# Gate tiles with the expert of a group innermost in place of the token

## The chip, the core and the metric

The kernel runs on one core of one Trainium2 chip. The metric is the device time of one execution, in microseconds (us). Three runs of the kernel before took 4170.88 us at the median, 4170.69 at the least and 4181.73 at the most.

## The reference

Two layers of a hybrid network run over 640 tokens of 1024 numbers (128 context tokens, 512 latent ones). Each layer has a mixer and then PEER, an expert layer with 16384 experts of one neuron each. For each token and each of 8 heads it takes the 16 best of all pairs of two keys (128 x 128 pairs are the 16384 experts), a softmax over these 16 gives the gates, and the output is a sum over the 128 chosen experts:

```
sv, si = lax.top_k(s, PEER_TOPK)                 # 16 best of 128 keys, for both halves
cand = sv[:, :, 0, :, None] + sv[:, :, 1, None, :]
fv, fpos = lax.top_k(cand, PEER_TOPK)            # 16 best of the 256 pairs
eidx = take_along_axis(cidx, fpos)               # number of the expert, i * 128 + j
g = softmax(fv)
act = gelu(einsum('td,ted->te', xb, u_tab[idx]))
out = einsum('te,ted->td', g * act, v_tab[idx])
```

## The kernel before, in words

PEER is done in two ways at once. For two tiles of 128 tokens the rows of `u` and `v` that the tokens chose are gathered from DRAM (`gather`, lines 1043 to 1065): an indirect DMA that GpSimd issues fetches 128 rows of 4 KB into one of four buffers `gb`, and VectorE takes a product with it or adds it to `acc`. For the other three tiles, 384 tokens, all 16384 experts are computed (`dense`, from line 1251): 128 blocks i of 128 experts j, each a product with `u` (tile `A`), a multiplication by the gates, and a product with `v`. Most gates are zero. The gathered rows are spread over the other stages in small portions, in the order in which the code is written, so that GpSimd, VectorE and the DMA queues work on them beside the matmuls.

The change is in the dense gates. The matrix of gates is 128 (j, on partitions) by 128 (i) by 384 tokens, in 16 groups of 8 blocks i. The first 4 groups (`NRES`) are kept in SBUF in the tile `Gt` (named `GT` in the code), the other 12 are spilled to the DRAM tensor `g_d` by way of the tile `Gs`, which has three buffers. Both have been laid out so far as group, block of 16 tokens, i in the group, token, the token innermost.

The gate stage (`gate`, lines 1210 to 1249) takes 16 tokens a step, in two halves of 8. For each half, TensorE makes `pj` and `pi` (lines 1222 and 1226), ScalarE and VectorE turn them into one-hot rows `OJ` and `OI` (lines 1223 and 1237; each fourth `OI` goes over ScalarE at line 1234 and GpSimd), and two groups of four products `pg` (line 1242) give the gates of four tokens each, a row of 128 numbers (over i) per token in PSUM. ScalarE evicts each group of four with two copies: 128 numbers into `Gt` (line 1244) and 384 into `Gs` (line 1246). It reads them in the order token, i. After 16 tokens SyncE issues the store of `Gs` to `g_d` (line 1248), 12 runs of 128 numbers on each partition. Beside it the last parts of the selection of other tiles run on VectorE and GpSimd (`late`, in the first 8 steps of the gate stage for one tile and in the first 9 steps of the dense stage for another), and one portion of gathered rows per half.

In the dense stage step i loads the weights, forms `A` for block i (`upd`), and for block i - 1 multiplies `A` by the gates (`mid`, lines 1277 to 1284), splits the product into a high part (ScalarE) and a low part (VectorE) in `wp`, and runs 18 matmuls with `v` (`down`, line 1293); `up` (line 1144) has 24. The product with the gates is line 1281, and a helper at line 77 records it:

```
av = A.rearrange("p (b t) -> p b t", t=16)
mul(av, av, GT[:, i // 8 % NRES, :, i % 8])
```

From the 32nd block on, a group of `Gt` that has been used is filled again from `g_d` (line 1259). In the last layer a used part of `Gt` holds rows of the output's gate (`final_rows`).

Each engine works through its instructions in the order in which the program lists them; the order is fixed when the program is built, and semaphores make an engine wait for another.

Of the kernel before, what the change touches and what calls it, by code (L numbers as in the profile page):

```python
# [20 lines left out]
D = 1024  # L21
# [22 lines left out]
def tile_kernel(ctx: ExitStack, tc: tile.TileContext, I, O, dbg=None, upto=99):  # L44
# [65 lines left out]
    # some columns of a modulation at a time: the weights stream past the two conditioning columns  # L110
# [50 lines left out]
    # pre: the first weights, split before  # L161
# [24 lines left out]
    # sums of the squares of the rows of xT, in two parts  # L186
# [12 lines left out]
    # 1 / rms of the tokens, on all partitions, in PSUM  # L199
# [78 lines left out]
    # an angle of any size modulo 2 pi, into [-pi, pi]  # L278
# [15 lines left out]
    # =========================== Hyena filters ===========================  # L294
    # Transforms at the odd frequencies 2 pi (f + 1/2) / 2L. For the latent tokens the even and the odd samples are
    # transformed apart, into E and O: what belongs to f is E + O, and the conjugate of what belongs to L - 1 - f
    # is E - O.
# [4 lines left out]
    # the discrete Fourier matrices come in two parts that float32r holds exactly  # L302
# [106 lines left out]
    # =========================== layer 0 mixer ===========================  # L409
# [19 lines left out]
    with ExitStack() as eq:  # L429
# [47 lines left out]
        # the input is read again after this: its place holds the convolved rows and the sum of the states  # L477
# [138 lines left out]
    # activations of one table follow each other  # L616
# [6 lines left out]
    def rglru(cp):  # L623
        # 4 softplus(-lambda), log1p by its atanh series
# [46 lines left out]
        def scans(d):  # L671
            for j in range(4):
# [3 lines left out]
                # q = (1 + a) / 2 = 1 / (1 + p), refined by one Newton step; its negative is kept  # L676
# [29 lines left out]
    # what the first direction of the S5 layer needs early  # L706
# [33 lines left out]
    with es, ExitStack() as eb:  # L740
# [6 lines left out]
        # the places of the convolved rows and of the states' sum are free again  # L747
# [76 lines left out]
        # what the chunks put out for four pairs of groups: from the chunk itself and from the state before it  # L824
# [88 lines left out]
    # =========================== PEER ===========================  # L913
# [7 lines left out]
    g_d = [dram.tile([16, 128, TD // 16, 8, 16], F32, name=f"g_d{l}") for l in range(2)]  # L921
# [34 lines left out]
    def peer(l):  # L956
# [5 lines left out]
        # the scores of two token tiles wait for their turn  # L962
# [22 lines left out]
        # one head of the n token tiles at slot s0: its 16 of the 54 pairs that can be among the largest  # L985
# [161 lines left out]
        # the first blocks of experts need no gates yet  # L1147
# [6 lines left out]
        GT = rp.tile([128, NRES, TD // 16, 8, 16], F32, name="Gt")  # L1154
# [19 lines left out]
        # dense gate matrix of a token tile: G[i][j, t], by one-hot products per token  # L1174
        # The numbers of a slot's two keys, each as digits a and b of 4 bits, make the row of a product whose
        # column c is 1 - (a - a_c)^2 - (b - b_c)^2: what is left above 0 is the one-hot row of the key.
# [33 lines left out]
        def gate(n, cr, gT, it, lt):  # L1210
            for tb in range(8):
                next(lt, None)
                Gs = kp.tile([128, 128 - 8 * NRES, 16], F32, name="Gs", tag="Gs", bufs=NGS)
                for t8 in range(2):
# [24 lines left out]
                    for t4 in range(2):  # L1239
# [4 lines left out]
                        S.copy(GT[:, :, tr, :, c0:c0 + 4].rearrange("p r i t -> p t r i"),  # L1244
# [6 lines left out]
        def dense(lp):  # L1251
# [25 lines left out]
            def mid(i):  # L1277
                A = st["A", i]
                WH, WL = wp[:, i % 2, 0], wp[:, i % 2, 1]
                av = A.rearrange("p (b t) -> p b t", t=16)  # L1280
                mul(av, av, GT[:, i // 8 % NRES, :, i % 8])
                S.copy(WH, A)  # L1282
                sub(WL, A, WH.bitcast(F32))
                st["W", i] = WH, WL
# [459 lines left out]
```

## Time and profile before

The profiled execution has a span of 4170.6 us, which is all that the profile gives as its own time; the three timed runs stand beside it.

| what | value |
|---|---|
| median of the runs | 4170.88 us |
| span of the profiled execution | 4170.6 us |
| TensorE matmul busy | 3630.2 us (87%) |
| VectorE busy | 3420.7 us (82%) |
| GpSimd busy | 2632.5 us (63%) |
| ScalarE busy | 1690.0 us (41%) |
| mean granted TensorE clock | 0.935 |
| DMA, mean over the span | 254 GB/s |

The shares are means over stages with different limits: the mixers, the selection, the gate stage and the dense stage. Engines are PE (TensorE matmul), PEld (its weight loads, which overlap the matmuls), DVE (VectorE), ACT (ScalarE), POOL (GpSimd) and SP (SyncE). What a number in the table is worth for the change is read from the stage in which the changed instructions run. The times of matmuls overlap, since one starts before the last has ended; so do those of ScalarE's and VectorE's instructions in part, and an instruction's duration is longer than the time for which it holds up the next.

### The profile page before, as it was taken

What the parts mean: (1) busy time and instruction counts of PE and PEld (TensorE: products, weight loads), DVE (VectorE), ACT (ScalarE), POOL (GpSimd) and SP (SyncE); (2) the same over time, 40 slices, a digit from 0 to 9 for tenths busy, and PEclk for the clock granted to TensorE, in tenths of its full rate; (3) what the DMA queues carried; (4) which work ended last, traced back from release to release, by engine and by line L of the source; (5) the groups of instructions that cost most, each with busy time, mean ns of one, the idle gap of its engine ahead of it and who ended that gap; (6) DMA issues with size and microseconds to landing.
All of it is one profiled execution on the core that took longest, in us unless ns stands there. A gap on an engine that the chain in (4) does not pass through costs nothing.

```text
span 4170.6 us, 57304 instructions
## 1 busy us (share of the span) xinstructions
PE 3630.2 (87%) x20066; PEld 3161.8 (76%) x20098; DVE 3420.7 (82%) x5990; ACT 1690.0 (41%) x3488; POOL 2632.5 (63%) x2178
## 2 busy tenths in 40 slices
PE   7868887488999999999789988843889999999997
PEld 4656873367898898998678778732678999999986
DVE  8872599989888888889865666999888888888888
ACT  3523435494333333333344333444843333333333
POOL 5631588757666666666655435887576666666675
PEclk9978998799999999999889999977999999999998
DMA  5564267698898999999724642656878999899997
GB/s 207 140 134 145 92 207 223 203 293 272 308 344 323 339 328 338 340 327 329 250 81 127 218 132 87 208 163 187 283 267 315 340 339 348 324 341 338 330 323 246
DMA packets 438105, 1057.42 MB, mean 254 GB/s; under 512 B 49175, under 2 KB 210967, under 8 KB 432696
## 3 DMA queue, kind: packets, MB, share of 16 engines
q0 software_dynamic: 152784, 555.55, 38.4%
q1 hardware_dynamic: 285032, 498.21, 35.5%
q8 instruction: 158, 2.59, 0.2%
q14 instruction: 131, 1.07, 0.1%
HBM read 993.86 MB, written 61.87 MB: 253 GB/s over the span
## 4 chain that ended last, share of the span: by engine, by line
PE 38%; DVE 26%; DMA 13%; issue 10%; POOL 7%; ACT 6%; SPq 1%; POOLq 0%; DVEq 0%; ACTq 0%
PE pso L1293 13%; PE pA L1144 12%; DMA gb<-in_peer_v,ei 8%; PE pproj L169 8%; DVE gb L1052 6%; POOL gb L1040 4%; DVE acc L95 3%; ACT Gs L1246 2%; DMA gb<-in_peer_u,ei 2%; PE pmod L129 2%; POOL jk L77 1%; DVE oh L77 1%; DVE ul L77 1%; ACT OJ L1223 1%; DVE tiu L976 1%
## 5 line engine op out<-in xcount | busy, mean ns | idle before, releaser
L1040 POOL DMA_INDIRECT gb<-in_peer_v,ei x512 | 687.9, 1343 | 435.0 <-DVE acc L95 335.6
L1293 PE MATMUL pso<-vh,wp 128*128 128x512 f32 x3072 | 883.3, 395 | 32.5 <-ACT wp L1282 23.9
L95 DVE SCALAR_TENSOR_TENSOR acc<-gb,pw,acc 128x1024 f32<-128x1024 f32 x508 | 774.4, 1524 | 137.0 <-DMA gb<-in_peer_v,ei 132.9
L1040 POOL DMA_INDIRECT gb<-in_peer_u,ei x512 | 636.0, 1242 | 391.3 <-DVE gb L1052 257.8
L1052 DVE SCALAR_TENSOR_TENSOR gb<-gb,hrow 128x1024 f32<-128x1024 f32 x512 | 756.1, 1481 | 100.8 <-DMA gb<-in_peer_u,ei 100.3
L1144 PE MATMUL pA<-hHd,uh 128*128 128x384 f32 x2048 | 691.6, 338 | 12.9 <-DVE modT L77 6.2
L1144 PE MATMUL pA<-hHd,ul 128*128 128x384 f32 x2048 | 691.6, 338 | 4.4 <-DVE ul L77 4.4
L1144 PE MATMUL pA<-hLd,uh 128*128 128x384 f32 x2048 | 690.0, 337 | 0.0
L1293 PEld LDWEIGHTS pso<-vh,wp 128*128 128x128 f32 x3072 | 575.1, 189 | 151.1 <-ACT wp L1282 29.5
L1293 PE MATMUL pso<-vl,wp 128*128 128x512 f32 x1536 | 486.8, 396 | 15.5 <-POOL vl L77 13.9
L1136 ACT CAST uh<-wraw 128x1024 fp32r<-128x1024 f32 x256 | 269.4, 1052 | 457.9 <-PE pA L1144 444.8
L1282 ACT CAST wp<-A 128x384 fp32r<-128x384 f32 x252 | 129.5, 514 | 781.1 <-DVE A L77 767.6
L1144 PEld LDWEIGHTS pA<-hHd,uh 128*128 128x128 f32 x2048 | 387.6, 189 | 24.3 <-DVE modT L77 6.2
L1144 PEld LDWEIGHTS pA<-hHd,ul 128*128 128x128 f32 x2048 | 387.3, 189 | 8.4 <-DVE ul L77 6.6
L1144 PEld LDWEIGHTS pA<-hLd,uh 128*128 128x128 f32 x2048 | 387.3, 189 | 8.2
L1293 PEld LDWEIGHTS pso<-vl,wp 128*128 128x128 f32 x1536 | 291.8, 190 | 83.2 <-POOL vl L77 15.2
L77 POOL TENSOR_TENSOR wl<-wraw,wh 128x1024 fp32r<-128x1024 f32 (+1 forms) x88 | 215.8, 2455 | 205.4 <-ACT wh L157 194.4
L77 DVE TENSOR_TENSOR ul<-wraw,uh 128x1024 fp32r<-128x1024 f32 x252 | 314.2, 1247 | 36.8 <-ACT uh L1136 33.5
L77 POOL TENSOR_TENSOR vl<-vraw,vh 128x1024 fp32r<-128x1024 f32 x128 | 332.3, 2596 | 15.8 <-ACT vh L1266 12.3
L1266 ACT CAST vh<-vraw 128x1024 fp32r<-128x1024 f32 x256 | 268.9, 1050 | 160.1 <-PE pso L1293 74.7
L1242 PEld LDWEIGHTS pg<-OI,OJ 128*128 128x128 f32 x1536 | 202.5, 202 | 112.4 <-POOL OI L77 42.8
L1242 PE MATMUL pg<-OI,OJ 128*128 128x128 f32 x1536 | 222.1, 292 | 43.9 <-DVE OI L1237 18.9
(537 smaller groups left out, 7020.1 us busy)
## 6 DMA issues: line engine op xcount, KB each, us to landing
wraw<-in_uT SPq DMA_DIRECT2D x256, 512.0 KB
vraw<-in_peer_v SPq DMA_DIRECT2D x256, 512.0 KB
g_d<-Gs SPq DMA_DIRECT2D x48, 768.0 KB
Gt<-g_d SPq DMA_DIRECT2D x24, 1536.0 KB
wmod<-in_w_mod SPq DMA_DIRECT2D x48, 512.0 KB
wraw<-in_wq SPq DMA_DIRECT2D x32, 512.0 KB
mw<-in_w_mod SPq DMA_DIRECT2D x16, 1024.0 KB
wraw<-in_w_in_c SPq DMA_DIRECT2D x24, 512.0 KB
```

The source lines that it names most:

```text
L77: (eng or V).tensor_tensor(o, a, b, op=op)
L95: V.scalar_tensor_tensor(o, a, s, b, op0=op0, op1=op1)
L129: PE.matmul(pm[:2, :cw], cond[:, k], w[k], start=k == 0, stop=k == 7)
L169: PE.matmul(p[:, i, :sg[2]], a[:, k, :], sg[hl](k), start=k == 0 and a is wh and hl == 0, stop=k == kk - 1 and a is wl)
L1040: G.indirect_dma_start(out=b, out_offset=None, in_=I[tab], in_offset=bass.IndirectOffsetOnAxis(ap=ei[:, s:s + 1], axis=0))
L1052: V.scalar_tensor_tensor(b, b, 1.0, hrow[:, i], op0=ALU.mult, op1=ALU.mult, accum_out=act[:, s:s + 1])
L1136: S.copy(uh, u)
L1144: PE.matmul(pA, a[:, k], b[:, k], start=k == 0 and b is hHd and a is uh, stop=k == 7 and a is ul)
L1242: PE.matmul(pg[:, t], OJ[:, t4 * 4 + t], OI[:, t4 * 4 + t], start=True, stop=True)
L1266: S.copy(vh, v)
L1282: S.copy(WH, A)
L1293: PE.matmul(pso[n][h], a[:, c], b[:, h * 512:(h + 1) * 512], start=i == 0 and a is WH and b is vh, stop=i == 127 and a is WL)
```

## The change

In `Gt`, `Gs` and `g_d` the last two dimensions change places: group, block of 16 tokens, token, i in the group. So the 8 numbers i of a group stand side by side for one token, where before 16 tokens stood side by side for one i. The two evictions read the same numbers in the same order and write them to the new places; they stand in a loop on one line now. The product with the gates reads its 384 numbers 8 places apart.

```diff
-    g_d = [dram.tile([16, 128, TD // 16, 8, 16], F32, name=f"g_d{l}") for l in range(2)]
+    g_d = [dram.tile([16, 128, TD // 16, 16, 8], F32, name=f"g_d{l}") for l in range(2)]
...
-        GT = rp.tile([128, NRES, TD // 16, 8, 16], F32, name="Gt")
+        GT = rp.tile([128, NRES, TD // 16, 16, 8], F32, name="Gt")
...
-                Gs = kp.tile([128, 128 - 8 * NRES, 16], F32, name="Gs", tag="Gs", bufs=NGS)
+                Gs = kp.tile([128, 16 - NRES, 16, 8], F32, name="Gs", tag="Gs", bufs=NGS)
...
-                        S.copy(GT[:, :, tr, :, c0:c0 + 4].rearrange("p r i t -> p t r i"),
-                               pg[:, :, :NRES * 8].rearrange("p t (r i) -> p t r i", i=8))
-                        S.copy(Gs[:, :, c0:c0 + 4].rearrange("p i t -> p t i"), pg[:, :, NRES * 8:])
+                        for o, a in ((GT[:, :, tr], pg[:, :, :NRES * 8]), (Gs, pg[:, :, NRES * 8:])):
+                            S.copy(o[:, :, c0:c0 + 4].rearrange("p r t i -> p t r i"),
+                                   a.rearrange("p t (r i) -> p t r i", i=8))
                     take(it, WSLOT[gi % len(WSLOT)])
-                nc.sync.dma_start(g_d[l][NRES:, :, n * 8 + tb].rearrange("g p i t -> p g (i t)"),
-                                  Gs.rearrange("p (g i) t -> p g (i t)", i=8))
+                nc.sync.dma_start(g_d[l][NRES:, :, n * 8 + tb].rearrange("g p t i -> p g (t i)"),
+                                  Gs.rearrange("p g t i -> p g (t i)"))
...
-                mul(av, av, GT[:, i // 8 % NRES, :, i % 8])
+                mul(av, av, GT[:, i // 8 % NRES, :, :, i % 8])
...
-            grow = GT[:, 0].rearrange("p b i t -> p (b i t)")[:, :2 * D].rearrange("p (s d) -> p s d", s=2)
+            grow = GT[:, 0].rearrange("p b t i -> p (b t i)")[:, :2 * D].rearrange("p (s d) -> p s d", s=2)
```

On TensorE, VectorE, GpSimd and SyncE the instructions stand in the same order before and after. On ScalarE they do too, with the evictions in another form. Before, a piece of ScalarE's order in the gate stage of layer 0 reads (`Gt` and `Gs` are the evictions, `OJ` and `OI` the one-hot rows):

```order
L1244 COPY Gt<-pg 128x4x4x8
L1246 COPY Gs<-pg 128x4x96
L1223 ACTIVATE OJ<-pj 128x1024
L1244 COPY Gt<-pg 128x4x4x8
L1246 COPY Gs<-pg 128x4x96
L1234 ACTIVATE OI<-pi 128x512
```

The same place after the change:

```order
L1245 COPY Gt<-pg 128x4x4x8
L1245 COPY Gs<-pg 128x4x12x8
L1223 ACTIVATE OJ<-pj 128x1024
L1245 COPY Gt<-pg 128x4x4x8
L1245 COPY Gs<-pg 128x4x12x8
L1234 ACTIVATE OI<-pi 128x512
```

Nothing has moved; `Gs` is written as 4 tokens by 12 groups by 8, and both evictions have one line.

## Rows read from the trace of the kernel before

**Rows 1.** Windows, gate stage: stretch, length, PE, PEld, DVE, ACT, POOL busy (count), clock, DMA share, GB/s.
```profile
763.00:863.00 100.00, 68.91 (x382) 51.73 (x389) 100.00 (x322) 60.78 (x109) 77.29 (x128) 0.86 0.63 191
880.00:938.00 58.00, 55.91 (x396) 44.16 (x401) 42.85 (x71) 58.00 (x111) 29.06 (x30) 1.00 1.02 328
...
2978.00:3030.00 52.00, 50.13 (x354) 39.55 (x359) 38.16 (x64) 52.00 (x100) 25.84 (x27) 1.00 1.03 321
```

**Rows 2.** Chain of waits, gate stage's second halves: start, duration, what.
```profile
865.02 0.65 ACT Gs L1246
...
938.65 1.07 ACT Gs L1246
...
2959.69 0.65 ACT Gs L1246
...
3030.71 1.05 ACT Gs L1246
```

**Rows 3.** Timeline of SyncE's queue, 880 to 940 us: first start, stretch, what, count.
```profile
879.92 58.40 SPq L1248 DMA_DIRECT2D g_d<-Gs  x11
```

**Rows 4.** Timeline of ScalarE, gate stage: start, duration, what.
```profile
897.92 0.51 ACT L1244 COPY Gt<-pg 128x128 f32<-128x128 f32 x1
...
898.75 0.76 ACT L1234 ACTIVATE OI<-pi 128x512 f32<-128x512 f32 x1
899.26 0.51 ACT L1244 COPY Gt<-pg 128x128 f32<-128x128 f32 x1
```

**Rows 5.** Timeline of TensorE, the same place.
```profile
897.69 1.05 PE L1242 MATMUL pg<-OI,OJ 128*128 128x128 f32 x8
898.58 0.59 PE L1222 MATMUL pj<-blk,cr 128*128 128x512 bf16 x2
```

**Rows 6.** Single lines, ScalarE's copies out of PSUM: duration in ns, min/median/max.
```profile
L1246 ACT COPY Gs<-pg x192: 801/902/1122, 770.7 to 3044.3; 128x384 f32<-128x384 f32 x192
...
L1103 ACT COPY sc<-psc x32: 451/479/509, 490.2 to 2753.5; 128x384 f32<-128x384 f32 x32
...
L1207 ACT COPY gT<-pgT x6: 246/258/273, 737.5 to 2943.3; 128x128 f32<-128x128 f32 x6
...
L466 ACT COPY uT<-pproj x8: 689/734/807, 127.1 to 175.7; 128x320 f32<-128x320 f32 x8
```

**Rows 7.** Single lines, TensorE's matmuls of the gate stage.
```profile
L1242 PE MATMUL pg<-OI,OJ x1536: 270/275/579, 769.3 to 3043.7; 128*128 128x128 f32 x192
...
L1222 PE MATMUL pj<-blk,cr x166: 376/379/634, 764.9 to 3031.5; 128*128 128x512 bf16 x166
```

**Rows 8.** Windows, dense stage, as rows 1.
```profile
950.00:1100.00 150.00, 134.51 (x629) 119.10 (x630) 139.18 (x195) 51.60 (x69) 116.28 (x99) 0.93 0.81 277
1100.00:1900.00 800.00, 793.30 (x3992) 719.36 (x3992) 680.09 (x746) 277.75 (x379) 508.66 (x335) 1.00 0.92 334
...
3730.00:3780.00 50.00, 50.00 (x254) 45.44 (x253) 44.88 (x60) 17.51 (x24) 31.17 (x22) 1.00 0.95 358
```

**Rows 9.** Groups by form, VectorE: total us, mean ns, idle before.
```profile
L77 DVE TENSOR_TENSOR A<-A,Gt 128x384 f32<-128x384 f32 x252 | 149.0, 591 | 0.1
...
L1017 DVE TENSOR_REDUCE ef<-jk 128x16 f32<-128x432 f32 x48 | 42.1, 877 | 2.0 <-POOL jk L77 2.0
...
L1026 DVE TENSOR_REDUCE gs<-gt 128x8 f32<-128x128 f32 x4 | 1.1, 278 | 0.3 <-ACT gt L1025 0.3
...
L1026 DVE TENSOR_REDUCE gs<-gt 128x24 f32<-128x384 f32 x2 | 1.1, 542 | 0.0
```

**Rows 10.** Waits, 950 to 2090 us: who for whom, us in total, times, longest.
```profile
DVE acc L95 <- DMA gb<-in_peer_v,ei: 63.1, 54, 4.5
...
PE pso L1293 <- ACT wp L1282: 13.4, 9, 4.6
```

**Rows 11.** Chain of waits through the run: products with the gates on it.
```profile
953.10 0.93 DVE Apre L77 x2
...
4129.60 0.56 DVE A L77
```

## The prediction

> **What bounds the kernel now.** I read the windows of busy time first, to find the stages in which the changed instructions run, then the chain of waits inside them, then the times of single instructions. The changed instructions run in two places of each PEER layer.
>
> The first is the gate stage (763 to 945 us in layer 0, 2862 to 3045 us in layer 1). It has two halves with different limits. In the first half VectorE is busy for the whole of its 100 us and ScalarE for 61 of them; in the second ScalarE is busy for 58.00 of 58 and 52.00 of 52 us, VectorE for under three quarters [rows 1]. The chain agrees: in the second half it runs through the evictions `Gs` on ScalarE, from 865.0 to 939.7 us and from 2959.7 to 3031.8 us [rows 2], 147 us in all. SyncE's stores give the pace there: 11 in a row, ten steps between 879.92 and 937.96 us, 5.80 us a step of 16 tokens [rows 3]. So 147 us are 25 steps whose pace ScalarE sets.
>
> The second place is the dense stage (950 to 2050 and 3036 to 4130 us). Its middle is TensorE's: 793 of 800 us busy, VectorE 680 [rows 8]. A step of one expert block has 42 matmuls, so the 3992 of that row are 95 steps of 8.4 us, in each of which VectorE is idle for 120 / 95 = 1.26 us. At the stage's beginning and end VectorE is tighter (139 of 150 us) [rows 8].
>
> **The change part by part.** No instruction, wait or transfer is added, removed or moved; each store still moves 12 runs of 128 numbers a partition. Two kinds of instruction get other strides.
>
> *The evictions.* For every 4 tokens ScalarE copies 512 numbers out of PSUM, 128 into `Gt`, 384 into `Gs`. Before, two numbers read one after another are written 64 bytes apart; now eight in a row are written together. Copies that write in a row take 258 ns for 128 numbers and 479 for 384: 0.86 ns a number over a base of 148. `Gs` takes 902 for the same 384, (902 - 148) / 384 = 1.96 a number, and `uT`, the other copy that scatters its writes, takes 734 for 320, 1.83 [rows 6]. What an instruction holds the engine for is read from its successor's start: `Gt` and `Gs` together 898.75 - 897.92 = 0.83 us, the 512-wide `OI` behind them, written in a row, 0.51 [rows 4]. If eight in a row are as good as a full row, ScalarE saves 4 x (0.83 - 0.51) = 1.28 us of the 5.80, and needs 4.5.
>
> What is late next? TensorE: eight product matmuls stand in 1.05 us with the last of 0.275 [rows 5, 7], so one starts every (1.05 - 0.275) / 7 = 0.111 us; two wide ones stand in 0.59 us, the last of 0.379, 0.211 apart [rows 5, 7]. [...] The DMA queues come close behind: the stretch moves 328 GB/s [rows 1], 1.90 MB a step. At the most that a 50 us stretch of this run moves, 358 GB/s, a step takes 5.31 us; at the 334 of the dense middle, 5.70 [rows 8], and 2.5 us are left of the gain. I take 5.45, between these two, nearer to the faster, since at 328 GB/s it is still ScalarE that is late here and no wait on a store: 0.35 x 25 = **9 us gained** (bounds 2.5 and 14). In the first half of the stage an eviction that is shorter gains nothing: VectorE has no idle time there, and ScalarE has 39 us of it.
>
> *The product with the gates.* In each dense step VectorE multiplies `A` by 384 gates. Before, it reads them in runs of 16; now each is 32 bytes from the last. No VectorE row of this trace reads at 32 bytes. The nearest is the reduction of `jk`, which reads at 64: 877 ns for 432 numbers, against 278 for 128 and 542 for 384 read in a row [rows 9]. In a row that is 1.03 ns a number over 146; strided, (877 - 146) / 432 = 1.69. Bounds: nothing, if a strided stream hides behind the other operand's, and, with the 1.10 ns a number that scattered writes cost ScalarE, 0.42 us. A gain I exclude, as the second operand is already read in runs. I take the reduction's, same engine and same side: 384 x 0.66 = 0.25 us, 591 ns becoming about 840. 256 of these are 64 us of VectorE.
>
> [...]
>
> How much of the 64 us shows? In the middle of the stage it lies in the 1.26 us that VectorE is idle a step, behind TensorE. That cover is mostly waits for gathered rows, 54 of them with 63 us in layer 0 [rows 10], whose transfers go on while the product takes longer. Where the cover is gone, the instructions behind the product on VectorE come late: the next gathered row's, and the low part of `wp` for TensorE. The chain through the whole run passes 38 of the 256 products, the first at 953.1, the last at 4129.6 us [rows 11], most of them at the ends of the two stages. 38 x 0.25 = **9.5 us lost**. With the bounds of the price: 0 to 16.
>
> Sum: -9 + 9.5 = +0.5 us on the profiled span of 4170.6 us. That span is 0.3 us under the median of the three runs (4170.88), and I find nothing outside it to add: 4171.4, so 4171.
>
> **The rivals.**
>
> *B: the strided read costs nothing.* For it: VectorE reads two operands, and only one is strided, while the reduction has one. Against it: its 1.69 ns a number is more than the 1.03 at which the other operand comes. Then only the gain is left: 4171 - 9 = 4162, and 4157 at the 14 us bound.
>
> *C: the transfers take the gain.* For it: the DMA share is already 1.02 in the stretch [rows 1]. `Gs` has three buffers, and a store that lands late holds up ScalarE's next eviction. Against it: no growing delay of the stores shows, they leave every 5.80 us from the first to the last. 2.5 us gained, 9.5 lost: 4178.
>
> *D, the other side: the product's length is not hidden in the dense stage.* Place: VectorE's queue between the product, the gathered rows' work and the low part of `wp`. For it: TensorE waits nine times for `wp` in layer 0 already [rows 10], and VectorE's idle time is waiting for rows that come late because their buffers were freed late; a product that lasts longer frees them later still. Against it: TensorE's 793 of 800 us. The tight ends are some 150 us at each end of each of the two stages, 600 us, 71 steps; if all of these pay, and a quarter of the other 185, it is 117 x 0.25 = 29 us, less 9: 4191. It decides from 86 products that pay (21.5 us, of which 9 are won back).
>
> *E: the evictions do not get faster*, because each run of eight still jumps by 512 bytes to the next. Against it: a run is eight numbers long, and no row with such runs stands in this trace. The loss alone: 4180.
>
> **How the numbers follow.** A change of 0.3%, 12.5 us, is about what a measurement of this kernel can tell from none. Forecast 0.48, B 0.17, C 0.13, D 0.16, E 0.06. The forecast's own range is 4163 to 4179. Faster than 4158.4 needs B with most of the 14 us (0.08), or the forecast with a product that mostly hides (0.03): 0.11. Slower than 4183.4 is most of D (0.13), and the tails of C, E and the forecast (0.04): 0.17. The rest, 0.72, is no change. The range from 4155 to 4190 leaves out the far ends of B and D.
>
> **What the changed profile would show.** Right: `Gs` near 480 and `Gt` near 260 ns where nothing queues; a store every 5.3 to 5.6 us in the second half of the gate stage, with ScalarE idle there and TensorE or a store ending its waits; the product near 840 ns; the dense middle as long as before, its ends some 2 us longer each. Wrong: a product still near 590 ns (B); a store step above 5.6 us with ScalarE waiting for `g_d` (C); TensorE's waits for `wp` doubled and the dense middles under 790 of 800 us busy (D); `Gs` still at 900 (E).

## The result, and the profile after

The changed kernel took 4195.68 us (median of 4 runs, 4189.05 to 4198.69), the kernel before 4170.78 beside it: a ratio of 1.0054, 95% interval 1.0039 to 1.0069, so some 22 us slower. The forecast was 4171 with 4155 to 4190. The profiled execution after spans 4192.9 us.

The windows of the kernel after come first; columns as in [rows 1].

```profile
763.00:863.00 100.00, 70.76 (x398) 53.43 (x399) 100.00 (x325) 50.38 (x110) 76.92 (x128) 0.87 0.65 193
880.00:938.00 58.00, 57.59 (x435) 50.29 (x433) 47.31 (x81) 51.93 (x119) 33.81 (x32) 1.00 1.04 348
2978.00:3030.00 52.00, 52.00 (x395) 45.82 (x394) 41.77 (x68) 47.40 (x110) 29.05 (x30) 1.00 1.06 357
...
950.00:1100.00 150.00, 133.69 (x619) 116.57 (x618) 142.13 (x170) 49.58 (x66) 119.50 (x94) 0.93 0.78 270
1100.00:1900.00 800.00, 783.85 (x3942) 710.32 (x3941) 708.67 (x741) 273.74 (x377) 538.85 (x331) 1.00 0.92 330
...
3180.00:3980.00 800.00, 789.39 (x3960) 714.77 (x3960) 709.81 (x744) 274.73 (x377) 528.78 (x332) 1.00 0.92 332
```

The last of these is the dense middle of layer 1; before the change it was

```profile
3180.00:3980.00 800.00, 796.99 (x4026) 724.23 (x4025) 682.44 (x753) 281.63 (x385) 509.94 (x336) 1.00 0.92 337
```

In the gate stage's second halves ScalarE has idle time for the first time (51.93 of 58 and 47.40 of 52 us), and TensorE has next to none (57.59 and 52.00 busy): the pace has passed to TensorE. In the first half VectorE is busy for all of its 100 us, as before. In the dense middle of layer 0 TensorE falls from 793.30 to 783.85 us of 800 and its matmuls from 3992 to 3942, while VectorE rises from 680 to 709 [rows 8]; in layer 1 the matmuls fall from 4026 to 3960. At 42 matmuls and 8.4 us a step these are some 10 and 13 us.

SyncE's queue after, in the gate stage of layer 0 (first start, stretch, what, count):

```profile
872.87 58.69 SPq L1248 DMA_DIRECT2D g_d<-Gs  x12
```

Twelve stores, so eleven steps of (58.69 - 0.36) / 11 = 5.30 us, the last issue taken off; before they were 5.80 [rows 3].

ScalarE's copies after (ns: least, median, longest), to be read beside `Gs` and `gT` in [rows 6]:

```profile
L1245 ACT COPY Gt<-pg x192: 246/265/367, 770.0 to 3043.8; 128x128 f32<-128x128 f32 x192
L1245 ACT COPY Gs<-pg x192: 478/485/606, 770.2 to 3044.0; 128x384 f32<-128x384 f32 x192
```

In runs of eight numbers the 384 of `Gs` are written in 485 ns, where they took 902 before and `sc` takes 479 in full rows [rows 6].

The product after, first in single lines, then with the reduction of `jk` in the groups by form (us in total, mean ns, idle before), beside [rows 9]:

```profile
L77 DVE TENSOR_TENSOR A<-A,Gt x252: 834/904/2996, 958.6 to 4159.4; 128x384 f32<-128x384 f32 x126
```

```profile
L77 DVE TENSOR_TENSOR A<-A,Gt 128x384 f32<-128x384 f32 x252 | 236.8, 940 | 0.1
L1017 DVE TENSOR_REDUCE ef<-jk 128x16 f32<-128x432 f32 x48 | 42.0, 875 | 0.0
```

The mean went from 591 to 940 ns; the median, which a few long ones of 2 to 3 us don't move, from 551 to 904, 0.353 us a block. A product of 192 gates in runs takes 351 ns (run_split, below) and one of 384 takes 551, so the base is 2 x 351 - 551 = 151 ns. A strided gate then costs (904 - 151) / 384 = 1.96 ns, more than the 1.69 of the reduction that the forecast took.

Waits after, 950 to 2090 us, beside [rows 10]:

```profile
DVE acc L95 <- DMA gb<-in_peer_v,ei: 58.7, 51, 3.7
...
PE pso L1293 <- ACT wp L1282: 20.4, 14, 3.7
...
PE pso L1293 <- DVE wp L77: 9.1, 9, 2.0
```

TensorE waits 14 times for the cast of `wp` where it waited 9 times, and 20.4 us in place of 13.4. VectorE's waits for the rows of `v` hardly shrank here (63.1 to 58.7 us), though the products in that stretch take some 44 us more (126 x 0.353). In layer 1 they shrank more. VectorE's waits for gathered rows there, first before (3040 to 4150 us):

```profile
DVE acc L95 <- DMA gb<-in_peer_v,ei: 69.8, 56, 3.9
DVE gb L1052 <- DMA gb<-in_peer_u,ei: 43.7, 28, 3.7
```

and after (3040 to 4170 us):

```profile
DVE acc L95 <- DMA gb<-in_peer_v,ei: 56.8, 51, 3.5
...
DVE gb L1052 <- DMA gb<-in_peer_u,ei: 32.6, 28, 3.3
```

With the rows of `u` in layer 0 (39.7 and 37.9 us), these waits come to 216 us in the two dense stages before and 186 after. So of some 89 us of longer products (252 x 0.353) they took up 30: that cover gave way only in part.

Last, the shares of the chain that ended last, by engine and by line, of the kernel before:

```profile
PE 38%; DVE 26%; DMA 13%; issue 10%; POOL 7%; ACT 6%; SPq 1%; POOLq 0%; DVEq 0%; ACTq 0%
PE pso L1293 13%; PE pA L1144 12%; DMA gb<-in_peer_v,ei 8%; PE pproj L169 8%; DVE gb L1052 6%; POOL gb L1040 4%; DVE acc L95 3%; ACT Gs L1246 2%; DMA gb<-in_peer_u,ei 2%; PE pmod L129 2%; POOL jk L77 1%; DVE oh L77 1%; DVE ul L77 1%; ACT OJ L1223 1%; DVE tiu L976 1%
```

and of the kernel after:

```profile
DVE 28%; PE 24%; DMA 20%; issue 14%; POOL 10%; ACT 3%; SPq 1%; POOLq 0%; DVEq 0%; ACTq 0%
DMA gb<-in_peer_v,ei 15%; PE pproj L169 7%; DVE gb L1052 6%; POOL gb L1040 6%; PE pso L1293 5%; PE pA L1144 5%; DVE acc L95 3%; DMA gb<-in_peer_u,ei 2%; PE pg L1242 2%; DVE ul L77 1%; PE pmod L129 1%; POOL vl L77 1%; DVE A L77 1%; DVE oh L77 1%; DVE OI L1237 1%
```

TensorE's share fell from 38 to 24%; gathered rows, their issue on GpSimd and VectorE's work on them (`gb`, `acc`) now hold 32%, against 22 before (the lines of `gb` and `acc`, summed before they are rounded). Once a chain can pass either through TensorE or through the gathers, a small delay moves it from one to the other, so these shares are a hint and not a price.

### The profile page after: what moved, and what is told of

The parts are those of the page before. It is cut to its first block, busy times and chain, and to the rows that moved or that the text cites. A ratio compares the mean times of both kernels' runs of the same rounds, so it can differ in the third digit from the quotient of the medians.

```text
span 4192.9 us, 57336 instructions
## 1 busy us (share of the span) xinstructions
PE 3632.5 (87%) x20098; PEld 3170.3 (76%) x20098; DVE 3522.3 (84%) x5990; ACT 1632.1 (39%) x3488; POOL 2713.3 (65%) x2178
## 3 DMA queue, kind: packets, MB, share of 16 engines
q14 instruction: 131, 1.07, 0.1%
## 4 chain that ended last, share of the span: by engine, by line
DVE 28%; PE 24%; DMA 20%; issue 14%; POOL 10%; ACT 3%; SPq 1%; POOLq 0%; DVEq 0%; ACTq 0%
DMA gb<-in_peer_v,ei 15%; PE pproj L169 7%; DVE gb L1052 6%; POOL gb L1040 6%; PE pso L1293 5%; PE pA L1144 5%; DVE acc L95 3%; DMA gb<-in_peer_u,ei 2%; PE pg L1242 2%; DVE ul L77 1%; PE pmod L129 1%; POOL vl L77 1%; DVE A L77 1%; DVE oh L77 1%; DVE OI L1237 1%
## 5 line engine op out<-in xcount | busy, mean ns | idle before, releaser
L1040 POOL DMA_INDIRECT gb<-in_peer_v,ei x512 | 731.7, 1429 | 424.0 <-DVE acc L95 326.3
L1040 POOL DMA_INDIRECT gb<-in_peer_u,ei x512 | 666.7, 1302 | 376.7 <-DVE gb L1052 240.3
L95 DVE SCALAR_TENSOR_TENSOR acc<-gb,pw,acc 128x1024 f32<-128x1024 f32 x508 | 795.0, 1565 | 119.0 <-DMA gb<-in_peer_v,ei 115.6
L1242 PEld LDWEIGHTS pg<-OI,OJ 128*128 128x128 f32 x1536 | 213.3, 207 | 87.5 <-POOL OI L77 38.3
```

The lines of the kernel that those rows point to most:

```text
L95: V.scalar_tensor_tensor(o, a, s, b, op0=op0, op1=op1)
L1040: G.indirect_dma_start(out=b, out_offset=None, in_=I[tab], in_offset=bass.IndirectOffsetOnAxis(ap=ei[:, s:s + 1], axis=0))
L1242: PE.matmul(pg[:, t], OJ[:, t4 * 4 + t], OI[:, t4 * 4 + t], start=True, stop=True)
```

## Experiments

Where a kernel of these has other gates or other rows, its expectation says so. Every ratio is to the kernel before, run beside it on the same chip.

### The two edits apart

```diff
# read_only, read_same: before, and
-                mul(av, av, GT[:, i // 8 % NRES, :, i % 8])
+                gv = GT[:, i // 8 % NRES].rearrange("p b i t -> p (b i t)").rearrange("p (b t n) -> p b t n", t=16, n=8)
+                mul(av, av, gv[:, :, :, i % 8])       # read_only
+                mul(av, av, gv[:, :, :, 7 - i % 8])   # read_same
# evict_only, evict_same: after, and
-                mul(av, av, GT[:, i // 8 % NRES, :, :, i % 8])
+                gv = GT[:, i // 8 % NRES].rearrange("p b t i -> p b (t i)").rearrange("p b (n t) -> p b n t", t=16)
+                mul(av, av, gv[:, :, i % 8])          # evict_only
+                mul(av, av, gv[:, :, 7 - i % 8])      # evict_same
```

In read_only and evict_only the numbers that the product reads hang on fewer of the evictions, and the order of instructions shifts; in the other two it is that of both kernels.

> The layout and the evictions of before; only the product with the gates reads 384 numbers 8 places apart (it takes other gates than the right ones). Theory 1, the loss is the longer product alone: product near 904 ns, gate stage as before, both dense stages longer by 17 to 21 us, time about 4171 + 38 = 4209 us. Theory 2, the loss in the dense stages comes in good part from what the faster gate stage brings forward (transfers and gathers that crowd later): the dense stages lose clearly less here, time 4185 to 4195. By the prediction's own step (38 products on the chain): 4171 + 13 = 4184.

> The layout and the evictions of after; the product with the gates reads its 384 numbers in runs of 16 (it takes other gates than the right ones). Theory 1: product 551 ns, gate stages shorter by about 5 and 11 us, nothing lost in the dense stages, time about 4171 - 15 = 4156. Theory 2: part of the gain is lost again in the dense stages, time 4165 to 4171.

> The kernel before with nothing changed but the product on VectorE, which reads its 384 gates eight numbers apart (in the opposite order of experts within a group, so it takes other gates than it should). The order of instructions on every engine is that of both kernels, so this is the price of the read without any other move. Product's median 900 to 910 ns as in the kernel after. Theory 1 (the two edits add: the loss sits in the dense stages and is paid by the read alone, the gain sits in the gate stages and is paid for by the evictions alone): as after minus the gate stages' 15 us of gain, 4171 + 38 = 4205 to 4212, that is slower by 0.8 to 1.0%. Rival (the gain of the gate stages was itself lost again, the dense stages starting with their gathers at another place): 4190 to 4197, no slower than after, and evict_same would then gain under 5 us.

> The kernel after with nothing changed but the product, which reads 384 gates in runs of 16 again (of other pairs, so it takes other gates than it should). The order of instructions on every engine is that of both kernels. Product's median 550 ns, evictions 478 and 246 ns as after. Theory 1 (the edits add): the gate stages keep their 15 to 17 us, so 4154 to 4157. Rival (the gain is given back by the gathers in the dense stages, whatever the product does): 4165 to 4172. An earlier kernel of the same edit with a slightly other order of instructions took 4148; if this one takes 4148 too, the order was of no account.

Measured: read_only 4197.53 us, 1.0056 (1.0036 to 1.0077); read_same 4205.79, 1.0084 (1.0068 to 1.0100); evict_only 4148.12, 0.9946 (0.9928 to 0.9963); evict_same 4159.40, 0.9967 (0.9953 to 0.9980). The product and an eviction in evict_same:

```profile
L77 DVE TENSOR_TENSOR A<-A,Gt x252: 543/551/2691, 960.6 to 4127.4; 128x384 f32<-128x384 f32 x126
...
L1245 ACT COPY Gs<-pg x192: 478/485/605, 772.1 to 3031.5; 128x384 f32<-128x384 f32 x192
```

and the product in read_same:

```profile
L77 DVE TENSOR_TENSOR A<-A,Gt x252: 832/911/3060, 961.7 to 4160.9; 128x384 f32<-128x384 f32 x126
```

read_same falls within its first expectation (4205 to 4212). evict_same lies 2 us above its first (4154 to 4157) and outside the rival's 4165 to 4172. read_only lies 3 us above its second (4185 to 4195) and far below its first (4209), and evict_only lies 8 us below its first. With the order held, the evictions alone gain 0.33% (14 us), the read alone loses 0.84% (35 us), and the sum, 21 us, is what the change costs (0.54%, 22 us). The edits add; the rival in which one eats the other falls. The two kernels in another order lie 12 us (read_only) and 9 us (evict_only) lower than their twins. The intervals of the twins overlap, so this is not clear of noise; but a shift of the instruction order that nobody intended may be worth as much as the effects looked for, and kernels below whose order shifts are read with a margin of some 10 us.

Where the 35 us fall is less plain. The dense middles of read_same, of layer 0 and of layer 1:

```profile
1095.00:1895.00 800.00, 793.33 (x3999) 719.53 (x3998) 720.84 (x748) 277.27 (x381) 534.49 (x334) 1.00 0.92 335
3180.00:3980.00 800.00, 790.43 (x3963) 712.66 (x3962) 715.26 (x741) 274.16 (x379) 546.00 (x330) 1.00 0.92 331
```

In this execution TensorE loses nothing in the middle of layer 0 (the kernel before has 793.30 us and 3992 matmuls from 1095 to 1895 us) and 63 matmuls in that of layer 1. VectorE's waits for gathered rows come to 164 us in the two dense stages, 52 less than before, for 252 x 0.360 = 91 us of longer products.

### From which step the read costs

```diff
# stride_mix: before, and
+                st_ = (1, 2, 4, 8)[i // 2 % 4]
+                gv = GT[:, i // 8 % NRES].rearrange("p b i t -> p (b i t)").rearrange("p (b t n) -> p b t n", t=16, n=st_)
-                mul(av, av, GT[:, i // 8 % NRES, :, i % 8])
+                mul(av, av, gv[:, 0:24, :, 0])
```

> The kernel before, with products that read every, every second, every fourth or every eighth number in turn by block (other gates than the right ones). If the price begins at 16 bytes: 551, 551, 904, 904 ns. If it grows with the step: four different times. Time between before and read_only.

A single run, 4195.86 us. The products sorted by their block's step, from the trace (60, 64, 64 and 64 of them): medians of 550 ns at a step of 4 bytes, 550 at 8, 835.5 at 16 and 908 at 32. Of these four steps 16 bytes is the first that costs, as its first expectation had it, but the 285.5 ns there are not yet the 358 of 32 bytes. What makes the difference between 8, 16 and 32 bytes is not shown.

### Half of the products strided

```diff
# read_half: before, and
-                mul(av, av, GT[:, i // 8 % NRES, :, i % 8])
+                gv = GT[:, i // 8 % NRES].rearrange("p b i t -> p (b i t)").rearrange("p (b t n) -> p b t n", t=16, n=8)
+                mul(av, av, gv[:, :, :, 7 - i % 8] if i // 2 % 2 else GT[:, i // 8 % NRES, :, i % 8])
```

> The kernel before with every second pair of blocks reading its gates eight numbers apart and the others in runs (the strided ones take other gates than they should); order of instructions that of both kernels. Half of the 0.353 us x 252 = 89 us is added. Theory 1 (each longer product costs by itself, as its own latency ahead of TensorE or as VectorE's time): half of what read_same loses, 15 to 20 us, 4186 to 4191. Rival (VectorE falls behind only where products come late in a row, and catches up in between): well under half, 4 to 9 us, 4175 to 4180.

4185.58 us, 1.0029 (1.0017 to 1.0041): 12 us, a third of read_same's 35, between the two expectations. The interval reaches from 7 to 17 us and so into both of them (4 to 9 and 15 to 20 us): half the dose costs something, and whether it costs half or less this run does not decide.

### The same time on VectorE in another instruction

```diff
# pre_two: before, and ahead of the product
+                scr = lp.tile([128, 176], F32, name="scr", tag="scr", bufs=1)
+                mul(scr, A[:, :176], A[:, 208:384])
# pre_one: in place of that mul
+                V.tensor_reduce(scr[:, :22], A[:, :176].rearrange("p (a b) -> p a b", b=8), axis=mybir.AxisListType.X, op=ALU.add)
# post_two: pre_two's two lines, behind this one
                 sub(WL, A, WH.bitcast(F32))
+                scr = lp.tile([128, 176], F32, name="scr", tag="scr", bufs=1)
+                mul(scr, A[:, :176], A[:, 208:384])
```

> The kernel before with a second VectorE instruction of some 0.33 us ahead of each product with the gates: a product of two operands of 176 contiguous numbers each, result unused. The product itself stays at 550 ns. The order of instructions on the engines shifts a little, as the longer queue is scheduled anew. Theory 1 (what costs is the time by which VectorE hands over the cast's operand later, whatever fills it): 256 x 0.33 us = 84 us of work, as read_same: 25 to 40 us longer, 4196 to 4211. Rival (what costs is the strided read as such, for instance by holding up GpSimd's issue of gathers or memory that others use): under 10 us, 4171 to 4181.

> pre_two with the extra VectorE instruction made a reduction of one operand (176 contiguous numbers, in eights) in place of a product of two; all else in the same order. If two operands at once on VectorE are what holds up GpSimd, and that is part of pre_two's 15 us, this one is at 4176 to 4182; if VectorE's time alone counts, it is at pre_two's ratio, 1.003 to 1.004 (4185 to 4190).

> The extra product of pre_two placed behind the subtraction that ends VectorE's part of a block, in place of ahead of the product with the gates. If what costs is the handing over of the block's operand to ScalarE and TensorE (the chain product, cast, subtraction), this is hidden: 4171 to 4177. If what costs is VectorE's time wherever it falls, as pre_two: 4185 to 4190.

Measured: pre_two 4187.44 us, 1.0036 (1.0021 to 1.0050); pre_one 4185.01, 1.0040 (1.0024 to 1.0056); post_two 4202.65, 1.0088 (1.0067 to 1.0108). pre_two lies between its two expectations (4171 to 4181 and 4196 to 4211), pre_one within its second. The two have the same order but for the exchanged instruction and cost the same within the noise, so no effect of the second operand on the time shows. post_two missed both of its expectations: behind the subtraction, where no operand of TensorE's in the same block waits for it, the same 0.33 us cost more, 37 us. What the three share is VectorE's time; the order of each is not that of before, so the 15, 17 and 37 us carry the margin of some 10. That margin does not cover the distance from the 15 us of pre_two to the 35 of read_same, at nearly the same time on VectorE (0.33 and 0.36 us a block), though read_only, whose order has shifted too, lies at 23. That VectorE's time alone sets the price is therefore not shown.

After pre_two I thought of GpSimd, whose gathers had become longer with the strided read and not with that filler. Of read_same (us in total, mean ns):

```profile
L1040 POOL DMA_INDIRECT gb<-in_peer_v,ei x512 | 744.3, 1454 | 397.7 <-DVE acc L95 295.0 <-DMA gb<-in_peer_v,ei 36.3 <-issue 35.8
L1040 POOL DMA_INDIRECT gb<-in_peer_u,ei x512 | 668.6, 1306 | 363.4 <-DVE gb L1052 238.5 <-issue 38.3 <-DVE tv L978 11.4
```

and of the kernel before:

```profile
L1040 POOL DMA_INDIRECT gb<-in_peer_v,ei x512 | 687.9, 1343 | 435.0 <-DVE acc L95 335.6 <-issue 36.3 <-DMA gb<-in_peer_v,ei 32.6
L1040 POOL DMA_INDIRECT gb<-in_peer_u,ei x512 | 636.0, 1242 | 391.3 <-DVE gb L1052 257.8 <-issue 40.7 <-DVE tv L978 13.7
```

The last columns of the kernel before already held what the forecast had missed: 335.6 + 257.8 us in which GpSimd could not issue the next gather until VectorE had worked on a row and freed its tile. In post_two the gathers are longer too:

```profile
L1040 POOL DMA_INDIRECT gb<-in_peer_v,ei x512 | 719.6, 1405 | 418.4 <-DVE acc L95 243.3 <-DVE scr L77 93.9 <-issue 31.3
L1040 POOL DMA_INDIRECT gb<-in_peer_u,ei x512 | 670.4, 1309 | 344.0 <-DVE gb L1052 162.1 <-DVE scr L77 61.5 <-issue 44.3
```

Here 93.9 + 61.5 us of GpSimd's waiting end with the filler `scr`, which stands behind the row's work. In total the issues take 1324 us before, 1413 in read_same, 1390 in post_two, but 1313 in pre_two and 1289 in pre_one. So the two kernels whose issues grew lose 35 and 37 us, and the two whose issues did not grow lose 15 and 17. This goes together; that the one causes the other is not shown.

### Gathers as plain transfers

```diff
# plain_before: before, and
-            G.indirect_dma_start(out=b, out_offset=None, in_=I[tab], in_offset=bass.IndirectOffsetOnAxis(ap=ei[:, s:s + 1], axis=0))
+            nc.sync.dma_start(b, I[tab][s * 128:(s + 1) * 128])
# plain_read: the same, with the product of read_same
```

> The kernel before, with each of the 1024 gathers of table rows replaced by a plain transfer of 128 rows that follow each other, issued by SyncE into the same ring of four tiles (so the latent tokens get other experts' rows). GpSimd issues no gathers any more; bytes into SBUF and VectorE's work on them stay. It is the base for plain_read. Without GpSimd's 1.3 us for a gather the ring turns faster: 4050 to 4165 us. Rival: SyncE, whose queue is in order, now waits for ring tiles ahead of the loads of weights, and the time rises to 4180 to 4300.

> plain_before with the product reading its gates eight numbers apart as in read_same (other gates); order of instructions that of plain_before. The product's median as in read_same, about 905 ns. Theory 1 (the 0.353 us are lost on VectorE itself, whose queue is late): plain_read loses against plain_before what read_same lost against before, 28 to 36 us. Theory 2 (they are lost because the product holds up GpSimd's issue of gathers, whose mean grew from 1343 to 1454 and from 1242 to 1306 ns in read_same and not in pre_two): under 12 us.

plain_before took 4068.48 us (0.9756, 0.9737 to 0.9775), plain_read 4087.28 (0.9791, 0.9770 to 0.9813): by the medians the read costs 19 us, by the ratios 15 (their quotient is 1.0036, about 1.0007 to 1.0065). In microseconds that interval is some 3 to 26: it leaves out theory 1's 28 to 36, and does not rule out theory 2's under 12. In the two profiled executions 7 of the 19 us were there before the first of the 252 products ran: it starts at 935.3 us in plain_before and at 942.4 in plain_read. Where the cost did not go is plain from the windows of plain_before

```profile
1095.00:1895.00 800.00, 800.00 (x4041) 727.61 (x4040) 667.78 (x761) 286.84 (x386) 134.89 (x48) 1.00 0.93 338
```

and of plain_read:

```profile
1095.00:1895.00 800.00, 800.00 (x4043) 727.93 (x4042) 724.36 (x759) 286.28 (x387) 137.99 (x48) 1.00 0.93 338
```

With rows that come when they are wanted the longer product is hidden entirely in the dense middle: VectorE takes 57 us more of 800, and TensorE does not lose one (in layer 1, 800.00 us both times, with 4060 and 4059 matmuls). What is left of the cost lies outside it. What VectorE waits for longest in this stretch, of plain_before

```profile
DVE ul L77 <- ACT uh L1136: 103.2, 70, 3.9
```

and of plain_read:

```profile
DVE ul L77 <- ACT uh L1136: 53.6, 38, 3.3
```

This is a wait for ScalarE's part of the next weights; rows make up 0.8 us of VectorE's idle time. The longer products took 50 us of it and delayed nothing. So the cover that the forecast counted on was real in this pair, where VectorE's idle time was not spent waiting for a gather. The plain transfers also take away GpSimd's issue, so this pair does not tell whether the ring costs by VectorE's lateness or by longer issues.

### Shorter instructions

```diff
# read_split: read_same, run_split: before, each with the product in two
# gv: the numbers that the product of read_same or of before reads
+                for c in range(0, 24, 12):
+                    mul(av[:, c:c + 12], av[:, c:c + 12], gv[:, c:c + 12])
```

> read_same with each product cut into two instructions of 192 gates (12 runs of tokens each), still eight numbers apart (other gates, as in read_same). VectorE is held longer than in read_same: two instructions of 150 + 192 x 1.96 = 526 ns in place of one of 905, some 0.13 us more a block, 33 us over the run; at the 15 us that 85 us of VectorE's time cost in pre_one, pre_two and plain_read this is 5 to 6 us. Theory 2 (GpSimd's issue of a gather waits out the VectorE instruction that starts with it, so half of the product makes it wait half as long, and the 20 us that read_same loses beyond VectorE's time go): gathers' means back to some 1340 and 1240 ns, 4187 to 4197. Theory 1 (only VectorE's time counts, and read_same's 35 us are all of that kind): 4205 + 13, that is 4212 to 4222, gathers as long as in read_same or longer.

> The kernel before with the product cut in the same two instructions, gates read in runs: the base for read_split, whose instruction order it has. Two instructions of 350 ns in place of one of 551, some 0.1 us of VectorE more a block, 25 us over the run. By VectorE's time 4 to 6 us longer than before, less what GpSimd's gathers gain from the shorter instructions: 4165 to 4178. Theory 1 has read_split 35 us or more above this one, theory 2 15 to 22.

read_split took 4199.24 us, 1.0063 (1.0046 to 1.0081), run_split 4158.96, 0.9969 (0.9958 to 0.9981). Both missed: read_split lies between its two expectations, run_split below the 4165 to 4178. The two have the same order, and the read costs 40 us between them, which is theory 1's 35 or more and not theory 2's 15 to 22. Their products, run_split first:

```profile
L77 DVE TENSOR_TENSOR A<-A,Gt x504: 342/351/2551, 968.3 to 4132.5; 128x192 f32<-128x192 f32 x168
...
L77 DVE TENSOR_TENSOR A<-A,Gt x504: 489/526/3203, 960.3 to 4161.9; 128x192 f32<-128x192 f32 x168
```

Gathers in run_split:

```profile
L1040 POOL DMA_INDIRECT gb<-in_peer_v,ei x512 | 681.1, 1330 | 444.6 <-DVE acc L95 337.0 <-DMA gb<-in_peer_v,ei 31.4 <-issue 29.2
L1040 POOL DMA_INDIRECT gb<-in_peer_u,ei x512 | 632.8, 1236 | 390.0 <-DVE gb L1052 265.0 <-issue 37.1 <-DVE tv L978 11.4
```

and in read_split:

```profile
L1040 POOL DMA_INDIRECT gb<-in_peer_v,ei x512 | 715.1, 1397 | 438.7 <-DVE acc L95 326.3 <-issue 37.3 <-DMA gb<-in_peer_v,ei 30.6
L1040 POOL DMA_INDIRECT gb<-in_peer_u,ei x512 | 640.1, 1250 | 384.4 <-DVE gb L1052 260.8 <-issue 34.8 <-DVE tv L978 11.4
```

Theory 2 falls as it was put: GpSimd's issues grow by (715.1 + 640.1) - (681.1 + 632.8) = 41 us here and by 89 us from before to read_same, and the loss is 40 and 35. The longer issue goes with the longer product, but does not set its price in proportion. That it has no part in the price is not shown: the means did not come back to the 1340 and 1240 ns that theory 2 asked for, and no run with gathers lengthens the product and leaves their issue as it was. That run_split is 0.3% faster than before, with more instructions on VectorE, is about what a shifted order may give, and is not explained here.

### A ring of three

```diff
# ring3_before: before, ring3_read: read_same, each with
-    NGB = 4
+    NGB = 3
```

> The kernel before with three tiles in the ring of gathered rows in place of four: the base for ring3_read. A gather is issued later, when a tile is free, so VectorE waits more for rows and TensorE for VectorE: 4200 to 4300 us.

> ring3_before with the product reading its gates eight numbers apart, as in read_same (other gates); the order of instructions is that of ring3_before. Theory 3 (a longer product costs where it delays the freeing of a ring tile: product, gathered row's work, free tile, GpSimd's issue, landing, VectorE again are one loop, and with fewer tiles more of the blocks have no slack in it): the loss against ring3_before is 45 to 80 us, over the 35 of a ring of four and the 15 to 19 of the ring that plain transfers fill faster. Rival (the loss is VectorE's queue ahead of TensorE alone, whatever the ring): 28 to 40 us.

ring3_before took 4482.54 us, 1.0740 (1.0719 to 1.0762), far over the 4200 to 4300 expected; ring3_read 4536.88, 1.0871 (1.0845 to 1.0896). The read costs 54 us, as theory 3 had it and outside the rival's 28 to 40 (the quotient of the ratios is 1.0122, about 1.009 to 1.015). The dense middle of ring3_before

```profile
1095.00:1895.00 800.00, 743.65 (x3559) 654.78 (x3558) 598.53 (x683) 244.61 (x341) 444.02 (x297) 0.96 0.84 299
```

and of ring3_read:

```profile
1095.00:1895.00 800.00, 728.11 (x3465) 638.90 (x3464) 616.32 (x664) 236.26 (x330) 459.60 (x288) 0.96 0.82 288
```

VectorE is idle for 201 us of 800 in ring3_before and for 132 in plain_before, where the longer product was hidden in the whole middle; here it costs TensorE 94 of 3559 matmuls (from 3180 to 3980 us, in layer 1, 9 of 3608). VectorE's longest waits from 1095 to 1895 us, of ring3_before

```profile
DVE gb L1052 <- DMA gb<-in_peer_u,ei: 100.2, 54, 5.5
DVE acc L95 <- DMA gb<-in_peer_v,ei: 85.3, 53, 4.4
```

and of ring3_read:

```profile
DVE gb L1052 <- DMA gb<-in_peer_u,ei: 98.1, 53, 5.6
DVE acc L95 <- DMA gb<-in_peer_v,ei: 72.6, 47, 4.8
```

These waits fell by 15 us only, where the wait for weights in plain_before gave 50. Idle time of VectorE that waits for the ring hid little in this pair. The ring of three also ran at a granted clock of 0.96 in this stretch, where before has 1.00; the two kernels compared have the same. By the tightness of the ring the same 0.36 us a block cost 15 to 19 us (plain transfers), 35 (four tiles) and 54 (three). Between the starts of the first and the last product in the profiled executions it is 11, 25 and 37 us. This supports the loop of the ring as the cause, whether by VectorE's lateness or by the longer issue within it: product, then the gathered row's work, then the free tile, GpSimd's issue, the landing, and VectorE again. The intervals of neighbours touch or nearly so; the ends of the series are apart.

### A layout between the two

```diff
# pairs: before, with gates laid out [.., 4 pairs, 16 tokens, 2 experts]
-        GT = rp.tile([128, NRES, TD // 16, 8, 16], F32, name="Gt")
+        GT = rp.tile([128, NRES, TD // 16, 4, 16, 2], F32, name="Gt")
-                mul(av, av, GT[:, i // 8 % NRES, :, i % 8])
+                mul(av, av, GT[:, i // 8 % NRES, :, i % 8 // 2, :, i % 2])
```

Evictions, `Gs` and the DRAM tensor follow the same layout.

> A third layout: the i of a group in pairs, two numbers i innermost, then 16 tokens. Evictions write two numbers (8 bytes) in a row, the product reads every second number (8 bytes apart). If a cost is paid only where two following accesses do not share 16 bytes: evictions near 480 and 265 ns as after, product near 551 ns as before, time about 4156 as with the evictions alone. If any step above one costs: product 650 to 900 ns, and 4165 to 4195. If runs of two are too short for the evictions: Gs 600 to 900 ns, time near 4171.

4156.84 us, 0.9972 (0.9959 to 0.9985), as its first expectation had it (about 4156), with the instruction order of before:

```profile
L77 DVE TENSOR_TENSOR A<-A,Gt x252: 543/550/2733, 958.3 to 4131.5; 128x384 f32<-128x384 f32 x126
...
L1246 ACT COPY Gs<-pg x192: 481/506/603, 770.7 to 3034.9; 128x384 f32<-128x384 f32 x192
```

Two numbers together are enough for both sides: the evictions are within 21 ns of those of the kernel after, and the product is that of the kernel before. It beats both kernels: 0.28% by the ratios, 12 us, about evict_same's 14.

## Why the prediction was wrong

- *The evictions.* Right in mechanism, short in size. `Gs` at 485 ns against 480, `Gt` at 265 against 260; the pace passed to TensorE at 5.30 us a step and not the 5.45 taken. The forecast's bound of 14 us is 25 x (5.80 - 5.24), and 5.24 us is an estimate from [rows 5, 7] for TensorE's matmuls of a step, 32 products `pg` at 0.111 and 8 wide ones at 0.211; no run shows a step of 5.24, and the 5.30 is close to it. The transfers kept up at 348 and 357 GB/s. 9 us were forecast; evict_same gains 14 (8 to 20), which was the bound.
- *The price of the read.* 0.353 us and not 0.25, within the bound of 0.42. ScalarE's scattered write was the nearer row, and the reduction on the same engine the wrong one: a strided gate takes 1.96 ns in all, ScalarE's figure, where the reduction has 1.69.
- *How much of it shows: this step failed.* The forecast let 38 of 256 products count, since 38 lay on the chain. 35 us at read_same's (911 - 551) = 0.360 us a product are 97. With the right price and the right gain, 38 products would still have given -14 + 38 x 0.353 = -1 us, no change; so it is the count that turned the sign, and the price only added to it. The sentence that fell is that VectorE's cover "is mostly waits for gathered rows", whose transfers go on while the product takes longer. These waits gave way only in part, by 30 us in the kernel after and 52 in read_same, of some 90 us of longer products. They stand at the end of a loop that runs through VectorE itself: GpSimd waits for VectorE to free a tile (335.6 + 257.8 us before), so later work on a row puts off a later row too. The three rings support this reading, without showing it block by block. And the loss did not stay at the ends: the dense middles, forecast as long as before, lost some 10 and 13 us in the kernel after. In plain_read, whose rows are there when wanted, the cover held in the dense middle; in ring3_read, where nearly all of VectorE's idle time waits for rows, it held least.
- *The rivals.* B (free) fell with the product's 904 ns (its 0.17 beside the forecast's 0.48 was the author's estimate), C (transfers) with the stores at 5.30 us, E with `Gs` at 485. D came true, in the place it named: dense middles 783.85 and 789.39 of 800 us, TensorE's waits for the cast in layer 0 up by half (not doubled), 97 products against its 117 and its deciding point of 86. That its 4191 comes near is in part luck: its count was too high, its price and the gain too low. Its "buffers freed late" was the argument that should have weighed more; rows for it stood in the trace of before, in GpSimd's idle time ahead of the gathers.
- *What stays open.* How the 35 us divide between lateness ahead of TensorE, the ring and the longer issue of gathers; why the same time on VectorE costs 15 us in pre_two and 37 in post_two, beyond the longer issues seen there; and what a shift of order is worth, which these runs only put at some 10 us.

## What to carry to other kernels

A chain of waits shows what was late once, not what has slack: before counting an engine's idle time as cover, look at what ends it, and if that is a ring which the same engine must free, do not count it in full. Here the time that was added showed for about a sixth with rows from plain transfers, two fifths with a ring of four and three fifths with a ring of three. Where a layout serves a writer and a reader, look for the shortest run that suits both (here two numbers of 4 bytes, with `Gs` at 506 ns and the product at 550) before moving the cost from one side to the other. Hold the instruction order when comparing effects of a third of a per cent.

## What the runs showed of the hardware that was not expected

- VectorE's product of 384 numbers takes 550 ns with one operand at a step of 4 or 8 bytes, 835.5 at 16 and 908 at 32 (stride_mix); in the kernel after a strided number costs 1.96 ns, the same as ScalarE's scattered write before the change.
- ScalarE's writes in pairs of 8 bytes, 128 apart from one pair of a token to the next, are nearly as fast as in runs of 32 bytes (506 ns in pairs and 485 after, for 384).
- Gathers' issues on GpSimd that started 0.03 to 0.15 us behind the start of a product lasted, by the medians of each run, 0.74 to 0.76 us longer than it. Of these issues between 950 and 4140 us the median took 1.09 us beside products of 0.35 (run_split), 1.28 beside 0.52 (read_split), 1.30 beside 0.55 (before) and 1.67 beside 0.91 (read_same); beside pre_two's filler, two operands in 0.33 us, it was 1.07. Beside pre_one's reduction of one operand in 0.32 us it was 0.94, hardly more than the shortest of all (0.93). So the issue's time went with that of a product of two operands and, in pre_one, not with that of a reduction of one; that it waits for the product is not shown, and pre_two and pre_one take the same time.
